# A table of distance biases: built on 8 or on 128 partitions, stored late or early

## The chip, the cores and the metric

The kernel runs on one core of a Trainium2 chip. The metric is the device time of one execution in microseconds (us), the median of several runs. A profile is one execution recorded by the hardware profiler; its span runs from the first to the last instruction of that execution. Engines are named as the profile names them: PE (TensorE matmuls), PEld (its weight loads), DVE (VectorE), ACT (ScalarE), POOL (GpSimd) and SP (SyncE, which issues nearly all DMAs; SPq in the rows is its queue).

## The reference, cut to what matters

Two transformer blocks run one after the other on 512 tokens of 1024 columns. The first has an attention branch with a distance bias:

```python
def first_block(x, ...):
    h = rms_norm(x, norm_gain)
    proj = h @ w_in                       # q, keys/values, gates, recurrent branch, merge gates
    y_a = nsa_mixer(q, k_cmp, v_cmp, k_slc, v_slc, k_win, v_win, br_gate, ..., rel_bias)
    y_b = rglru_mixer(...)
    return x + merge(y_a, y_b) @ w_out

def nsa_mixer(...):                       # 8 heads in 2 groups of 4, blocks of 128 queries
    # compressed, selected and window branch, each:
    s = einsum(q, k) + rel_bias[t5_bucket(dist)]      # dist = query position - key position
    p = masked_softmax(s, dist >= 0)                  # a key ahead of the query takes no part
    ...
```

`rel_bias` is a table of 32 buckets by 8 heads. A bias depends on the head and on the distance alone. The second block (a gated recurrence, differential attention and a mixture of 32 experts) reads `x` of the first.

## The kernel before, in words

Products are in float32, each as three products of operands split into a high part and a rest (`h`/`l`, 24 matmuls of 512 columns for a [128, 512] result). Weights come in tiles of 512 KB: `gr` (wa, wo), `gt` (wb), `ada_w` (the second block's modulation), `cw` (compression), later `wg` and `wd` of the experts; ACT or DVE make the high part (`gth`, `grh`) and DVE or POOL the rest (`gtl`, `grl`).

The instructions are first recorded in a plain order, by `block1`, `block2` and `moe`, and then issued in an order that a planner (`Plan.order`) sets: by a simple table of durations, each engine takes the first recorded instruction that is ready. So the place in the plain order is a priority, not a place in time. Every engine then runs its own list in order and stops at an instruction whose operand is not there. All instructions are issued by one line of `Plan.issue`, so every row of the profile says L409; rows are told apart by the names of tiles.

The plain order of the first block: `hT_first` (the hidden states and the q product), `qkv(0)` (q normalised and transposed), `compress_in`, `qkv(1)` (keys and values), `bias_tables`, `nsa_gates`, `compress`, and then four rounds r = 0 to 3 of `silu2`, `bias(r)` and `nsa(r)`, two heads each; after these the recurrent branch.

`bias_tables` (line 830) makes, for each head, a row of 640 negated biases over all distances: a matmul of `rb` (32 buckets by 8 heads) with `oh` (a one-hot table of bucket by distance), in two pieces, and on DVE the negated sum with `far` (1e30 where the key lies ahead). The row stands on 8 partitions (`tab`, a tile of the size class t4). One DMA from these writes it to DRAM (`Rd`, [8, 128, 640]) 128 times per head, a copy for each query of a block. `bias(r)` reads it back with rows of 639 elements apart, so that each query's copy is shifted by one: `B`, [128 queries, 512 keys], one DMA for each of the 8 heads. From `B` DVE makes `cbias` (the bias of the compressed keys) and adds `B` to the scores of both other branches (`P<-b,B`).

A DMA of SP waits until the DMA that was issued eight before it has landed. A tile of a size class waits for the last use of the tile that had its buffer.

Of the kernel before, what the change touches and what calls it, by code (L numbers as in the profile page):

```python
# [47 lines left out]
class View:  # L48
    """A part of a planned tile: a stand-in access pattern, and the steps to it from the whole tile."""
# [45 lines left out]
    def box(self):  # L95
        """partitions, range of elements and, where the tile has rows, range in a row."""
# [31 lines left out]
class Offset:  # L128
    """Row offsets of an indirect DMA."""
# [49 lines left out]
class Plan:  # L179
    """Records the instructions of a program in a plain order, then issues them in an order in which every  # L180
    engine, by a simple model of its speed, always takes the first recorded instruction that is ready.  A tile
    is taken ahead of the plain order only where its tag has a buffer to spare up to its place in it."""
# [24 lines left out]
    @contextmanager  # L207
    def together(self):
        """the instructions of the body, all on one engine, stay in one piece."""
        self.grouped = []  # L210
        yield
        g, self.grouped = self.grouped, None
        self.record([(g[0][0][0][0], [x[0][0][1:5] for x in g], None, None, None, sum(x[0][0][5] for x in g), None, False)],
                    [v for x in g for v in x[1]], [v for x in g for v in x[2]])

    def record(self, alts, writes, reads, load=False):
# [9 lines left out]
        for v in reads:  # L226
# [5 lines left out]
            if v.t.space == "psum":  # L232
                # engines take turns at a bank
                deps.update(k for _, k in v.t.reads if len(alts) + len(k.alts) > 2 or k.alts[0][0] != alts[0][0])
# [230 lines left out]
def shares(eng, meth, outs, ins):  # L465
    """whether an instruction holds the ports of the SBUF that DVE and Pool share: Pool's that read it, DVE's with
    two inputs from it, and those that use both of its ports for one."""
# [8 lines left out]
def price(self, eng, meth, args, kw):  # L476
    """Nanoseconds that an instruction holds its engine, roughly."""
# [30 lines left out]
class Net:  # L508
# [16 lines left out]
    SIZES = {"t4": 38, "a2": 15, "p2": 9, "vm": 4, "sq128": 3, "c1k": 4}  # L525

    def start(self):
        """a plan for the instructions that follow; tiles kept by the one before stay where they are."""
# [48 lines left out]
    def pair4(self, name):  # L577
        """four [128, 512] operands of split products."""
# [9 lines left out]
    def slab(self, src, name="w", scale=None):  # L588
        """[128, 1024] of weights: high part and rest; scale: factors of 512 columns."""
# [13 lines left out]
    def mm3(self, ps, pairs, byk=False):  # L603
        """ps = sum over (lhs hi, lhs lo, rhs hi, rhs lo)."""
# [11 lines left out]
    def rsqrt(self, v, n, scale, out=None):  # L616
        """v -> (v * scale + EPS) ** -0.5 on [p, n], in a new small tile or in out."""
# [25 lines left out]
    def constants(self):  # L643
# [11 lines left out]
        # the table of functions, ahead of the data  # L655
# [12 lines left out]
    def load_rows(self, src, name):  # L668
        """the four chunks of rows."""
# [5 lines left out]
    def norm_rows(self, x):  # L675
        """x * rstd, token major."""
# [8 lines left out]
    def new_hT(self, src=None):  # L685
        """hidden states, transposed and split; src: 32 more columns, multiplied on the way."""
# [7 lines left out]
    def hT_first(self):  # L694
        """the hidden states of the first block, without 1 / rms: those factors (r1 per token, R as a row on all
        partitions) go to what is computed from them."""
# [52 lines left out]
    def scaled(self, out, ps):  # L749
        """out = ps / rms in the first block, ps in the second."""  # L750
# [36 lines left out]
    def narrow(self):  # L787
        """the 32 more columns, token major: psum [128, (chunk, 32)]."""
# [8 lines left out]
    def gemm_t(self, src, name="gt"):  # L797
        """columns on partitions: psum [128 cols, 512 tokens]."""
# [7 lines left out]
    def group(self, src, name="gr", scale=None):  # L806
        """split operands of 512 columns; src [4, 128, 1024] (pairs of k tiles)."""
# [6 lines left out]
    def gemm_part(self, ps, grp, c, lhs_hi, lhs_lo, ks):  # L814
        """adds the products of k tiles ks to ps."""
# [6 lines left out]
    def gemm_r(self, grp, c, lhs_hi, lhs_lo, byk=False):  # L822
        """tokens on partitions: psum [128 tokens of chunk c, 512 cols]."""
# [6 lines left out]
    def bias_tables(self):  # L830
        nc, I = self.nc, self.I
        oh, R = self.t4("tab0")[:32, 0:640], self.t4("tab1")[:8, 0:640]
        nc.sync.dma_start(oh, I["oh"])
        rb = self.small([32, 8], "rb", bufs=1)
        nc.sync.dma_start(rb, I["rel_bias"])
        nc.sync.dma_start(R, I["far"].to_broadcast([8, 640]))
        for a, b in ((0, 512), (512, 640)):
            p = self.pst()
            nc.tensor.matmul(p[:8, :b - a], rb, oh[:, a:b], start=True, stop=True)
            nc.vector.scalar_tensor_tensor(R[:, a:b], p[:8, :b - a], -1.0, R[:, a:b], op0=OP.mult, op1=OP.add)  # L840
        # a row per query, so that rows of one less read as shifted
        Rd = self.tile("dram", [8, 128, 640], F32, "Rd")
        nc.sync.dma_start(Rd, R.unsqueeze(1).to_broadcast([8, 128, 640]))
# [6 lines left out]
    def bias(self, r):  # L850
        """negated bias of the two heads of r, [query of a block, key], and that of the compressed keys."""
# [16 lines left out]
    def qkv(self, grp, acc=None, W=None):  # L868
        """q (grp 0) or the keys and values (grp 1): normalised, transposed; values token major."""
# [121 lines left out]
    def silu2(self, ps, name):  # L991
        """2 * silu of a psum tile."""
# [8 lines left out]
    def split_into(self, hi, lo, src, scale):  # L1001
        """hi + lo = src * scale."""
# [4 lines left out]
    def cmp_attention(self, r):  # L1007
        """weights over the compressed keys, times the gate, transposed: [(chunk % 2, g, key), (chunk // 2, query)]."""
# [73 lines left out]
    def lru_setup(self):  # L1082
# [7 lines left out]
        # softplus(-lambda)  # L1090
# [48 lines left out]
    def conv(self, up, wname, bname, i, nt):  # L1139
        """causal depthwise convolution along the tokens of a [128, 512] tile."""  # L1140
# [9 lines left out]
    def log1p(self, out, y, z, q):  # L1150
        """out = log1p(y) for y in [0, 1]; z, q scratch."""
# [10 lines left out]
    def gate_tile(self, wg, i):  # L1162
        """tanh(x / 2) of one tile of merge gates."""
# [8 lines left out]
    def merge(self, wg, g0, wp, a_hi, a_lo, b_hi, b_lo):  # L1172
        """sigmoid gates over two projections, split for the output product."""
# [25 lines left out]
    def block1(self):  # L1199
        nc, I = self.nc, self.I  # L1200
        self.qT, self.kT, self.V, self.mg = [], [], [], {}
        self.qkv(0, self.hT_first())
        self.compress_in()
        self.qkv(1, W=self.group(I["wa1"][1]))
        self.bias_tables()
# [35 lines left out]
    def modulation(self):  # L1241
        """One step per row tile of w_ada; the sections are shift1, scale1, gate1, shift2, scale2, gate2."""
        nc, I = self.nc, self.I
        for s in (1, 0, 2, 4, 3, 5):
# [11 lines left out]
            # sums over the partitions: four groups of 32 equal rows, 256 columns each  # L1256
# [29 lines left out]
    def conv_silu2(self, idx, i):  # L1286
        """2 * silu(conv(.)) of column tile idx."""
# [10 lines left out]
    def prefix(self, p, tri, ones, v, n):  # L1298
        """sums over the tokens up to each one; v [128, (chunk, n)]."""
# [6 lines left out]
    def mgates(self):  # L1306
        """per token and head: a = i - F, exp(-(F + M)); and the rows of M."""
# [83 lines left out]
    def rope_tables(self):  # L1391
        """cos and sin of position * inv_freq, [128, 4 chunks, 8]."""
# [33 lines left out]
    def qk_diff(self, grp, wname, scale, name):  # L1426
        """rms-normalised, rotated, transposed; one [128 = 2 maps x 64, 512] tile per head."""
# [36 lines left out]
    def diff(self, qT, kT, vd, after):  # L1464
        nc = self.nc
        # lam
# [125 lines left out]
    def route_setup(self):  # L1592
        """router weights with the modulation in them, and what the shift adds to the logits."""
# [27 lines left out]
        # per token: its number, weights over the experts  # L1621
# [16 lines left out]
    def route_chunk(self, c, h, x):  # L1638
        """half of the columns of x2 of a chunk: transposed for the router; with the second half, its logits."""
# [29 lines left out]
    def rest_chunk(self, c):  # L1669
        """what the high part leaves of the normalised rows."""  # L1670
# [10 lines left out]
    def route(self, lo, hi):  # L1681
        """group, two experts of it and their weights, per token of some chunks; places in the order of the tokens."""
# [8 lines left out]
        # first place of the largest group logit  # L1691
# [232 lines left out]
def layout(a):  # L1924
# [63 lines left out]
    for m in range(512):  # L1988
        oh[_bucket(dist)[m], m] = 1.0
# [18 lines left out]
```

## Time and profile before

| | us |
|---|---|
| runs (3) | 1157.68, 1158.07, 1160.14; median 1158.07 |
| span of the profiled execution | 1157.3 |
| PE busy in it | 1080.1 (93%) |
| DVE / ACT / POOL busy | 653.8 / 405.3 / 189.7 |
| DMA, mean over the span | 188 GB/s |

The profile gives the span as that execution's own time. It lies 0.8 us under the median of the runs, and what an execution has around its span is not shown apart. PE's busy time includes matmuls that wait in its pipeline, so 93% is not 93% of PE's peak. The section on rows below names what is read from the trace.

### The profile page before, as it was taken

The numbers are of one execution on the slowest core, as the hardware profiler recorded it, in microseconds if no ns is written. First come the engines' busy times: TensorE is split into PE (matmuls) and PEld (weight loads), VectorE is DVE, ScalarE is ACT, GpSimd is POOL, SyncE is SP. The second block draws the span as 40 slices with busy tenths as digits, with TensorE's granted clock in tenths as the row PEclk, the third lists the DMA queues.
The fourth block names the chain that finished last, engine by engine and source line by source line (L and its number), as shares of the span: only waits on it lengthen the run. The fifth ranks groups of instructions, "written<-read, shape, count | busy, mean of one in ns | idle before, by whom it ended". The sixth has DMA issues, their size and how long they took to land.

```text
span 1157.3 us, 15019 instructions
## 1 busy us (share of the span) xinstructions
PE 1080.1 (93%) x5414; PEld 757.7 (65%) x5414; DVE 653.8 (56%) x1459; ACT 405.3 (35%) x824; POOL 189.7 (16%) x180
## 2 busy tenths in 40 slices
PE   7994299999999999999999999999999999999995
PEld 6773167777788777777677887788787444444431
DVE  4841288989656474776978786544717322333221
ACT  6320166756222243634663342222325111111120
POOL 2300033200111122420130201100204101111011
PEclk9996599999999999999999999999999999999998
DMA  9635810113443471815044322545966999999981
GB/s 346 227 88 87 247 46 20 37 56 95 131 143 119 163 255 53 296 37 220 10 158 157 129 86 73 178 131 156 354 264 219 349 387 363 371 385 367 389 292 26
DMA packets 74506, 217.22 MB, mean 188 GB/s; under 512 B 10820, under 2 KB 12428, under 8 KB 74424
## 3 DMA queue, kind: packets, MB, share of 16 engines
q1 hardware_dynamic: 72120, 211.98, 52.5%
q0 software_dynamic: 2304, 4.20, 2.1%
q8 instruction: 45, 0.74, 0.3%
q14 instruction: 37, 0.30, 0.1%
HBM read 204.56 MB, written 15.22 MB: 190 GB/s over the span
## 4 chain that ended last, share of the span: by engine, by line
PE 60%; DMA 14%; issue 11%; DVE 9%; SPq 2%; ACT 2%; another core or an unknown queue 1%; POOL 0%; POOLq 0%; DVEq 0%; ACTq 0%
PE b L409 59%; DMA out_rows<-Y,si 11%; SPq L409 2%; PE H L409 1%; DVE P L409 1%; DVE dP L409 1%; DMA gr<-in_wo 1%; DMA gr<-in_wa 1%; DMA B<-Rd 1%; DVE ada_acc L409 1%; ACT grh L409 1%; DVE grl L409 1%; DVE dq L409 0%; DVE uc L409 0%
## 5 line engine op out<-in xcount | busy, mean ns | idle before, releaser
L409 PE MATMUL b<-hTh,gth 128*128 128x512 f32 x464 | 124.5, 404 | 0.0
L409 PE MATMUL b<-hTh,gtl 128*128 128x512 f32 x464 | 121.1, 399 | 0.0
L409 PE MATMUL b<-hTl,gth 128*128 128x512 f32 x464 | 119.3, 395 | 0.0
L409 PE MATMUL H<-wg,XT 128*64 128x512 f32 x512 | 114.8, 596 | 0.0
L409 PEld LDWEIGHTS b<-hTh,gth 128*128 128x128 f32 x464 | 86.8, 190 | 22.2 <-issue 3.5
L409 PEld LDWEIGHTS b<-hTh,gtl 128*128 128x128 f32 x464 | 87.0, 189 | 20.5 <-issue 1.6
L409 PEld LDWEIGHTS b<-hTl,gth 128*128 128x128 f32 x464 | 86.4, 188 | 19.4 <-issue 0.9
L409 POOL TENSOR_TENSOR gtl<-gt,gth 128x1024 fp32r<-128x1024 f32 x23 | 56.4, 2455 | 247.0 <-ACT gth L409 222.4
L409 PEld LDWEIGHTS H<-wg,XT 128*64 128x64 f32 x512 | 35.0, 137 | 68.5 <-issue 59.5
L409 DVE SCALAR_TENSOR_TENSOR ada_acc<-ada_w,cols,ada_acc 128x1024 f32<-128x1024 f32 x42 | 60.3, 1435 | 7.5 <-DMA ada_w<-in_w_ada 7.5
L409 POOL DMA_INDIRECT out_rows<-Y,si x16 | 25.0, 1563 | 236.0 <-DVE Y L409 203.0
L409 PE MATMUL b<-grh,hTh 128*128 128x512 f32 x192 | 57.1, 410 | 6.0 <-ACT grh L409 6.0
L409 PE MATMUL b<-kT,qT 64*128 64x128 f32 (+3 forms) x128 | 26.4, 515 | 36.0 <-DVE nst L409 35.9
L409 PE MATMUL b<-wd,aT 128*64 128x512 f32 x256 | 58.4, 598 | 1.5 <-ACT aT L409 1.5
L409 ACT ACTIVATE gth<-gt 128x1024 fp32r<-128x1024 f32 x54 | 56.4, 1049 | 6.7 <-DMA gt<-in_wb 6.6
L409 DVE SCALAR_TENSOR_TENSOR act<-act,H 128x256 f32<-128x256 f32 x32 | 13.4, 420 | 79.6 <-ACT act L409 79.1
L409 PE MATMUL b<-grl,hTh 128*128 128x512 f32 x192 | 57.0, 405 | 0.0
L409 POOL TENSOR_TENSOR grl<-gr,grh 128x1024 fp32r<-128x1024 f32 x15 | 39.4, 2635 | 100.0 <-ACT grh L409 87.6
L409 ACT ACTIVATE P<-P,nst 128x128 f32<-128x128 f32 (+3 forms) x64 | 35.3, 553 | 57.2 <-DVE nst L409 57.0
L409 PE MATMUL b<-grh,hTl 128*128 128x512 f32 x192 | 55.3, 400 | 0.0
L409 DVE SCALAR_TENSOR_TENSOR Y<-b,wt,gate 128x512 f32<-128x512 f32 x32 | 24.0, 750 | 49.8 <-PE b L409 49.4
L409 DVE TENSOR_TENSOR gtl<-gt,gth 128x1024 fp32r<-128x1024 f32 x35 | 42.6, 1222 | 14.8 <-ACT gth L409 13.1
(380 smaller groups left out, 1973.6 us busy)
## 6 DMA issues: line engine op xcount, KB each, us to landing
wg<-in_wgu SPq DMA_DIRECT2D x128, 512.0 KB
wd<-in_wd SPq DMA_DIRECT2D x128, 256.0 KB
gt<-in_wb SPq DMA_DIRECT2D x58, 512.0 KB
ada_w<-in_w_ada SPq DMA_DIRECT2D x48, 512.0 KB
gr<-in_wa SPq DMA_DIRECT2D x23, 512.0 KB
wp<-in_wp SPq DMA_DIRECT2D x16, 512.0 KB
gr<-in_wo SPq DMA_DIRECT2D x16, 512.0 KB
cw<-in_cmp_w SPq DMA_DIRECT2D x8, 512.0 KB
```

What stands on the lines that cost most here:

```text
L409: i = getattr(getattr(self.nc, eng), meth)(*[val(a) for a in args], **{k: val(v) for k, v in kw.items()})
```

## The change

The table of biases is built on 128 partitions, 16 equal rows for each head. A DVE copy spreads `rb` to `rx` (32 buckets by 128 = 8 heads x 16), one matmul of `rx` with 512 columns of `oh` gives all 128 rows, DVE negates them into `tab`, and POOL fills the other 128 columns of `tab` with 1e30, in place of a second matmul and the `far` table. The store then goes out from 128 partitions, eight copies from each. `Rd` and its readers are unchanged. `bias_tables` is recorded right after `hT_first`, ahead of `qkv(0)`. The rest of the diff takes out comments and docstrings, which emit nothing.

```diff
     def bias_tables(self):
         nc, I = self.nc, self.I
-        oh, R = self.t4("tab0")[:32, 0:640], self.t4("tab1")[:8, 0:640]
-        nc.sync.dma_start(oh, I["oh"])
+        oh, R = self.t4("tab0")[:32, 0:512], self.t4("tab1")[:, 0:640]
         rb = self.small([32, 8], "rb", bufs=1)
         nc.sync.dma_start(rb, I["rel_bias"])
-        nc.sync.dma_start(R, I["far"].to_broadcast([8, 640]))
-        for a, b in ((0, 512), (512, 640)):
-            p = self.pst()
-            nc.tensor.matmul(p[:8, :b - a], rb, oh[:, a:b], start=True, stop=True)
-            nc.vector.scalar_tensor_tensor(R[:, a:b], p[:8, :b - a], -1.0, R[:, a:b], op0=OP.mult, op1=OP.add)
-        # a row per query, so that rows of one less read as shifted
+        nc.sync.dma_start(oh, I["oh"])
+
+        rx = self.sq128("rx")[:32, :]
+        nc.vector.tensor_copy(rx.rearrange("p (h i) -> p h i", i=16), rb.unsqueeze(2).to_broadcast([32, 8, 16]))
+        p = self.pst()
+        nc.tensor.matmul(p, rx, oh, start=True, stop=True)
+        nc.gpsimd.memset(R[:, 512:640], BIG)
+        nc.vector.tensor_scalar(R[:, 0:512], p, -1.0, None, op0=OP.mult)
+
         Rd = self.tile("dram", [8, 128, 640], F32, "Rd")
-        nc.sync.dma_start(Rd, R.unsqueeze(1).to_broadcast([8, 128, 640]))
+        nc.sync.dma_start(Rd.rearrange("h (i r) m -> (h i) r m", r=8), R.unsqueeze(1).to_broadcast([128, 8, 640]))
         self.Rd = Rd
...
     def block1(self):
...
-        self.qkv(0, self.hT_first())
+        acc = self.hT_first()
+        self.bias_tables()
+        self.qkv(0, acc)
         self.compress_in()
         self.qkv(1, W=self.group(I["wa1"][1]))
-        self.bias_tables()
```

In the host layout `oh` shrinks to 512 columns and `far` goes. Since the planner orders anew, other instructions move too, on every engine, up to the recurrent branch; from there on the lists are the same.

On SP the store stood behind the weights of the attention rounds, with the first `B` eight issues later and `vbd` (values of the compressed keys) behind it. Before:

```order
L409 DMA gt<-in_wb 128x1024
L409 DMA Rd<-tab_276 1024x1x640
L409 DMA gt<-in_wb 128x1024
L409 DMA ada_w<-in_w_ada 128x1024
L409 DMA gt<-in_wb 128x1024 x2
L409 DMA ada_w<-in_w_ada 128x1024
L409 DMA gt<-in_wb 128x1024 x2
L409 DMA B_766<-Rd 128x512
L409 DMA B_779<-Rd 128x512
L409 DMA vbd<-vbd 64x128
```

Now it stands among the compression's weights, ahead of the copies of `kcT`, and four `B` stand ahead of the first weights of the rounds:

```order
L409 DMA wd<-in_wd 128x512
L409 DMA Rd<-tab_78 1024x1x640
L409 DMA cw_406<-in_cmp_w 128x1024
L409 DMA kcS<-kcT 64x512 x2
L409 DMA cw_440<-in_cmp_w 128x1024
L409 DMA cw_469<-in_cmp_w 128x1024
L409 DMA kcS<-kcT 64x512 x2
L409 DMA B_518<-Rd 128x512
L409 DMA B_533<-Rd 128x512
L409 DMA B_559<-Rd 128x512
L409 DMA B_575<-Rd 128x512
L409 DMA b_627<-in_cmp_b 64x256 x2
```

So the store moved ahead of three `cw`, four `gt` and one `ada_w`, and of the four copies `kcS`; the reads of `Rd` moved ahead of all weights of the rounds, and `vbd` (not in the rows) moved behind seventeen of these, `gt` and `ada_w`.

On DVE the first reader of `B` stood behind all of the compression and the first gate (`gn`). Before:

```order
L409 COPY kcT<-b 128x64
L409 TENSOR_TENSOR sx<-b,R 128x512
L409 SCALAR_TENSOR_TENSOR gn_829<-gn_829,sx 128x512
L409 TENSOR_SCALAR cbias<-B_766 128x7
L409 TENSOR_SCALAR cbias<-B_766 128x15
```

Now it stands ahead of the last sums of squares (`ssq_qk`) of the keys and of the first rests of `gt`:

```order
L409 TENSOR_REDUCE ssq_qk<-sqk 128x4
L409 TENSOR_TENSOR blk_162<-kcT,cols 64x8x31
L409 TENSOR_SCALAR cbias<-B_518 128x7
L409 TENSOR_SCALAR cbias<-B_518 128x15
L409 TENSOR_SCALAR cbias<-B_518 128x23
L409 TENSOR_SCALAR cbias<-B_518 128x31
L409 TENSOR_SCALAR cbias<-B_533 128x7
L409 TENSOR_SCALAR cbias<-B_533 128x15
L409 TENSOR_SCALAR cbias<-B_533 128x23
L409 TENSOR_SCALAR cbias<-B_533 128x31
L409 TENSOR_REDUCE ssq_qk<-sqk 128x4
L409 TENSOR_TENSOR gtl<-gt,gth 128x1024 x2
```

So a late `B` would now hold up DVE before the keys are normalised, where before it held up DVE behind them.

## Rows read from the trace of the kernel before

**Rows 1.** The page: busy time of PE, and its chain by line.

```profile
PE 1080.1 (93%) x5414; PEld 757.7 (65%) x5414; DVE 653.8 (56%) x1459; ACT 405.3 (35%) x824; POOL 189.7 (16%) x180
...
PE b L409 59%; DMA out_rows<-Y,si 11%; SPq L409 2%; PE H L409 1%; DVE P L409 1%; DVE dP L409 1%; DMA gr<-in_wo 1%; DMA gr<-in_wa 1%; DMA B<-Rd 1%; DVE ada_acc L409 1%; ACT grh L409 1%; DVE grl L409 1%; DVE dq L409 0%; DVE uc L409 0%
```

**Rows 2.** Waits from 0 to 300 us: total us, times, longest us.

```profile
DVE cbias L409 <- DMA B<-Rd: 44.1, 1, 44.1
...
PE b L409 <- DVE nst L409: 35.9, 1, 35.9
```

**Rows 3.** Chain of work, 90 to 140 us: start us, us, what.

```profile
89.88 11.31 PE b L409 x45
...
126.84 9.53 DMA B<-Rd
...
136.40 0.43 DVE cbias L409 x4
```

**Rows 4.** SP's timeline, 0 to 140 us: start us, us, DMA issued, times.

```profile
55.27 1.10 SPq L409 DMA_DIRECT2D gt<-in_wb  x1
72.90 0.82 SPq L409 DMA_DIRECT2D Rd<-tab  x1
73.82 5.40 SPq L409 DMA_DIRECT2D gt<-in_wb  x1
79.31 18.16 SPq L409 DMA_DIRECT2D ada_w<-in_w_ada  x1
...
126.84 1.58 SPq L409 DMA_DIRECT2D B<-Rd  x2
```

**Rows 5.** Stretches: length, busy us (instructions) by engine, clock, DMA share, GB/s.

```profile
core 0: us, PE busy (x) PEld busy (x) DVE busy (x) ACT busy (x) POOL busy (x), PEclk, DMA share, GB/s
101.20:137.10 35.90, 0.02 (x1) 0.02 (x1) 0.70 (x7) 0.04 (x1) 0.00 (x0) 0.53 0.69 159
90.00:97.00 7.00, 7.00 (x28) 5.41 (x28) 1.38 (x2) 0.63 (x1) 0.00 (x0) 0.52 0.46 50
137.10:144.90 7.80, 7.80 (x28) 5.12 (x29) 6.12 (x38) 5.26 (x21) 2.68 (x7) 0.52 1.01 392
20.00:40.00 20.00, 20.00 (x96) 15.64 (x95) 9.80 (x11) 12.98 (x20) 11.27 (x7) 1.00 0.83 314
```

**Rows 6.** Instructions of tile `tab`: duration ns min/median/max, first and last start us, forms.

```profile
L409 PE MATMUL b<-tab,rb x4: 267/428/591, 70.6 to 71.6; 32*8 32x512 f32 x2, 32*8 32x128 f32 x2
L409 DVE SCALAR_TENSOR_TENSOR tab<-b,tab x2: 269/474/679, 71.7 to 72.6; 8x512 f32<-8x512 f32 x1, 8x128 f32<-8x128 f32 x1
```

**Rows 7.** Timelines of DVE, POOL, PE and ACT, 23 to 73 us, with idle time ahead.

```profile
25.14 1.23 DVE L409 TENSOR_TENSOR gtl<-gt,gth 128x1024 fp32r<-128x1024 f32 x1 [6.31 <-ACT gth L409]
...
34.27 0.68 DVE L409 COPY R<-b 128x512 f32<-128x512 f32 x1
...
37.34 1.21 DVE L409 TENSOR_TENSOR grl<-gr,grh 128x1024 fp32r<-128x1024 f32 x1
...
49.11 0.65 PE L409 MATMUL b<-ident,qtok 128*128 128x128 f32 x4 [1.40 <-DVE qtok L409]
...
66.24 2.01 ACT L409 ACTIVATE gth<-gt 128x1024 fp32r<-128x1024 f32 x2
...
72.28 0.40 DVE L409 TENSOR_REDUCE ssq_qk<-sqk 128x4 f32<-128x256 f32 x1
```

**Rows 8.** Stretches ahead of, in and behind the four rounds; columns as in rows 5.

```profile
60.00:73.00 13.00, 13.00 (x61) 9.82 (x61) 4.53 (x9) 5.01 (x11) 0.00 (x0) 1.00 0.14 57
...
88.00:90.00 2.00, 0.82 (x3) 0.43 (x3) 1.35 (x2) 0.00 (x0) 1.04 (x1) 0.99 0.47 51
137.10:157.80 20.70, 20.70 (x132) 13.87 (x132) 15.29 (x77) 14.16 (x47) 5.55 (x12) 0.82 0.55 206
157.80:218.00 60.20, 56.49 (x456) 40.16 (x452) 54.66 (x215) 40.67 (x114) 19.69 (x19) 1.00 0.04 10
880.00:1157.00 277.00, 259.16 (x1230) 117.64 (x1229) 91.29 (x220) 50.34 (x121) 32.08 (x26) 0.99 0.89 321
```

More of the change, by code (lines that the diff above doesn't have):

```diff
@@ L1984, in layout @@
     d["rows"] = np.concatenate([rows[k].reshape(-1) for k in ROWS])[None, :]
-    dist = 511 - np.arange(640)
-    oh = np.zeros((32, 640), np.float32)
-    for m in range(512):
-        oh[_bucket(dist)[m], m] = 1.0
+    oh = np.zeros((32, 512), np.float32)
+    oh[_bucket(511 - np.arange(512)), np.arange(512)] = 1.0
     d["oh"] = oh
-    d["far"] = np.where(dist < 0, np.float32(BIG), np.float32(0)).astype(np.float32)[None, :]
     return {k: np.ascontiguousarray(v) for k, v in d.items()}
```

## The prediction, made before the changed kernel ran

> **What bounds the kernel now.** The page shows PE busy for 93% of the span, and its chain is PE for more than half of its length, with B<-Rd, the read of the bias table, as an entry of its own [rows 1]. A kernel like this gets shorter only where PE stands still or runs slowly, so I looked at the waits next. In the first 300 us one wait stands out on two engines: DVE waits 44.1 us, once, for B<-Rd, and behind DVE PE waits 35.9 us, once [rows 2]. The chain says where: PE's work ends at 101.2 us, B lands at 136.4, and the first thing that DVE does then is cbias [rows 3]. SP's timeline says why. The store of the table (Rd<-tab) is issued at 72.9 us and the first read of it not before 126.8; the read needs the whole store landed, so the store takes about 126.8 - 73.7 = 53 us. The loads behind it crawl too (one issue takes 18.16 us) [rows 4]. From 90 to 97 us, with the store the main traffic, DMA moves 50 GB/s at a share of 0.46, about eight of sixteen engines; in two stretches of loads to 128 partitions it moves 314 and 392 GB/s [rows 5]. 2560 KB (2.62 MB) in 53 us is 49 GB/s, the same number. So the wait is the store's own slowness and its late issue. In the stretch from 101.2 to 137.1 no engine does anything worth naming [rows 5]: all of them are behind B.
>
> [...]
>
> **The change part by part.** The table itself. Before: two matmuls (their four entries, two of 512 and two of 128 columns, sit between 70.6 and 71.8, some 1.2 us of PE) and two DVE operations of 0.68 and 0.27 us [rows 6]. After: one matmul of 512 columns, by the same rows at most two entries of about 0.43, 0.86 us, so PE gains 0.3 us; one DVE negation of 128x512, priced by R<-b of the same form at 0.68 us [rows 7]; a DVE copy 32x128, between zero and that 0.68, and a POOL fill while POOL has nothing that others wait for. The DVE copy waits for rb, and behind it stands the first rest gtl, which waited 6.31 us for its own data anyway, until 25.14 [rows 7]. rb is queued ahead of that weight, so the copy is covered; if rb came later than that, each us would go straight to gtl. The two small loads rb and oh move ahead of two gt and four gr on SP: some 65 KB, 0.2 us of DMA at 314 GB/s, and less than before in all, since far is gone.
>
> The negation stands on DVE behind R<-b (34.27) [rows 7], and a grl of 1.21 us moves from POOL to DVE [rows 7], about 1.9 us more on DVE ahead of the normalised q. Against that four blk operations, which stand ahead of qtok now, move behind it, and with them the wait for kcS. PE waits 1.40 us at 49.11 for qtok [rows 7]. I take that wait as gone (-1.4); the bounds are 0.5 us of extra wait (1.9 less 1.4) and the whole 1.4 won.
>
> The store. It can be issued when the table is there, at about 36 us, and SP's loads ahead of it are done by about 37. Its duration is not in this trace; the bounds are the 53 us of now, at 49 GB/s, and 2.62 MB at 392 GB/s, 6.7 us. I take 8.3 us (314 GB/s, the rate of loads to 128 partitions at that time) [rows 5], since the new store spreads over 128 partitions as they do. Some 13 MB have been asked for ahead of it, at 314 GB/s 41 us, an estimate; so it lands near 50, and B for the first rounds, four reads of 256 KB behind it, by about 58. Who is behind it: the copies kcS and two cw, needed by operations that do not reach PE until 72.8; on SP, behind the four B, the biases of the compression and three gt, the first of which was needed at 66.24 by ACT [rows 7]. Loads end at 56 us today and SP is then idle to 72.9 [rows 4], so all of this has some 5 to 10 us of cover. If the store takes more than about 20 us, the cover is gone. cbias on DVE now stands ahead of ssq_qk and gtl, at about 60 us, and DVE has cover there: from 60 to 73 it is busy for 4.53 of 13 us [rows 8].
>
> The wait. With B there by 58, DVE can start the first round as soon as its scores are there, about 91 us. What is late next is PE itself. The two pieces of PE's work, 89.88 to 101.2 [rows 3] and the first round from 137.1 to 157.8 [rows 8], now stand together: the 35.9 us between them go. The second period at the lower clock goes too: 7.8 us at 0.52 would be 4.1 at full clock, 3.7 us less. The first one stays, since what comes ahead of it is unchanged.
>
> In that joined piece PE has fewer finished scores to work on. Its bounds: no wait at all, as in the round from 137.1 (PE busy 20.70 of 20.70), or waits as in the three later rounds, 60.2 - 56.49 = 3.7 us in three [rows 8]. I take 1 us. vbd stands behind 17 loads on SP now. Most of their buffers come free when the products of the keys end, where the bias matmuls start now, at 70.6 [rows 6]; vbd is wanted near 100, so I take zero.
>
> The sum: -35.9 - 3.7 - 1.4 - 0.3 + 1.0 = -40.3 us. The profiled execution would go from 1157.3 to 1117.0, and with the 0.8 us to the median, about **1118 us**. Everything behind is the same list, moved ahead: in the experts' stretch DMA is at a share of 0.89 [rows 8], but those loads wait for buffers, not for a time of day.
>
> [...]
>
> **The rivals.** *Only twice as fast*: each engine's pace is what limits the store (49 GB/s by eight engines, 6.1 each), so sixteen give 98 GB/s and 27 us. It lands near 66, B near 70. DVE stands at cbias until then; the gt behind B land near 74, their gtl ends near 78 instead of 70, and kT comes about 5 us later: 1123. For it: nothing shows that a partition and not an engine is slow. Against: the same engines carry 314 GB/s in loads.
>
> *As slow as before, only earlier* (the repeated rows, not the partitions, are slow): 53 us from 37 is 90, B at 93. DVE stands at cbias from 61 to 93; from ssq_qk (72.28) to the first round (about 90.5, from PE's 89.88) it has 18 us to go [rows 3, 7], so the first round starts near 113 instead of 137. But the 11 us of PE work from 90 to 101 are then still to do, and the weights behind B on SP come late (3 us more): 1157.3 - 24 + 11 + 3, near 1147.
>
> *The gain is swallowed later*: if the stretch of the experts, 277 us at 321 GB/s [rows 8], ran at a pace that started when it does now, nothing would be won: 1158. Against it: its loads wait for buffers that the earlier work frees.
>
> *Slower than before*: the lower clock holds through the rounds. It fell after two us with PE busy for 0.82 of them, and the new order puts few long matmuls between the softmax steps of the first round. In the four rounds PE is busy 77.2 us, of which 69.4 at full clock [rows 8]. Each us of these at half clock costs one us; from 41 us on (more than half of them) the change loses, and at the most it would be 1118 + 69 = 1187. Against it: the later rounds with their own waits hold 1.00 [rows 8].
>
> **How the numbers follow.** Forecast 0.80 (1107 to 1131), only twice as fast 0.09 (1123), as slow as before 0.03 (1147), swallowed 0.03 (1158), slower 0.04, rest 0.01. The range: at the low end, 9 us more if the first slow period (3.4), the wait from 88 to 90 (1.2) and the later rounds' waits (3.7) went too: 1109, less 2 for what the new order may save. At the high end, 1118 + 5 (second case) + 4 (waits in the joined piece) + 2 (wait for qtok, and its gain not had) + 2 for a read B of the second round that comes late behind its buffer: 1131. A measurement of this kernel can tell about 0.2% from no change (2.3 us). Faster: 0.80 + 0.09 + 0.03 + 0.01 = 0.93; same 0.03; slower 0.04.
>
> **What would show it.** Right: Rd<-tab issued near 37 us and the first B<-Rd within 15 us of it; no wait of DVE for B above 2 us; PE without a hole between 90 and 140; one period of lower clock in the first round, not two; a DMA share near 0.9 while the store runs. Wrong: a store that takes 25 us or more, with DVE idle ahead of cbias between 61 and 95; ssq_qk or kT later than 80 us; PE's clock at 0.5 in the later rounds; a gap in front of the experts that was not there.

## The result, and the profile after

The changed kernel takes 1127.1 us (median of 4 runs, 1123.0 to 1129.2) against 1159.1 us for the kernel before (1157.7 to 1161.5): a ratio of 0.971, 95% interval 0.969 to 0.973. The forecast was 1118, with a range from 1107 to 1131. So the sign and the range held, but of the 40.3 us of the sum 32.1 came in the profiled run (span 1157.3 before, 1125.2 after). Most of what follows is about the 8 us that are missing.

The profile page of the changed kernel answers [rows 1]: PE's share rises from 93% to 96%, and `B<-Rd` is no longer in the chain.

```profile
PE 1081.7 (96%) x5412; PEld 758.1 (67%) x5412; DVE 655.3 (58%) x1465; ACT 404.7 (36%) x827; POOL 182.7 (16%) x172
...
PE 65%; DMA 12%; issue 11%; DVE 8%; ACT 1%; POOL 1%; POOLq 0%; SPq 0%; ACTq 0%; DVEq 0%
```

SP's timeline (start us, us, what, times) answers [rows 4]. The store is issued at 35.6 us and the first read of its result at 48.9, so it takes at most 13 us in the thick of the weight loads.

```profile
35.57 0.64 SPq L409 DMA_DIRECT2D Rd<-tab  x1
...
48.92 2.07 SPq L409 DMA_DIRECT2D B<-Rd  x4
```

PE's waits from 0 to 300 us (total us, times, longest) answer [rows 2]. The 35.9 us are gone, and so is the wait for qtok of [rows 7]; what is left in the rounds is many small waits.

```profile
PE b L409 <- ACT grh L409: 6.2, 1, 6.2
PE b L409 <- DVE sc L409: 2.3, 2, 1.2
...
PE b L409 <- DVE PT L409: 1.6, 3, 0.6
PE b L409 <- POOL P L409: 1.2, 1, 1.2
```

The table by stretches (length, busy us of each engine with instructions, clock, DMA share, GB/s) answers [rows 5, 8]. DMA moves 327 GB/s while the store runs. The granted clock is at 0.50 once at the start of the first round, as forecast, and then again from 178 to 184 us, in the last round, where the kernel before had 1.00 throughout.

```profile
40.00:50.00 10.00, 10.00 (x53) 8.34 (x52) 8.59 (x21) 0.00 (x0) 0.00 (x0) 1.00 1.02 327
90.00:92.00 2.00, 2.00 (x12) 1.80 (x13) 1.09 (x3) 0.65 (x4) 0.31 (x1) 0.50 0.00 0
...
178.00:180.00 2.00, 1.61 (x7) 1.05 (x8) 1.95 (x5) 0.65 (x2) 1.43 (x1) 0.50 0.00 0
...
182.00:184.00 2.00, 2.00 (x9) 1.48 (x7) 1.40 (x4) 0.94 (x3) 0.01 (x1) 0.50 0.50 92
```

One more low stretch lies behind the rounds, at the products of the experts (length, PE busy, clock, DMA share, GB/s):

```profile
1096.00:1098.00 2.00, 2.00 (x8) 0.50 0.00 0
```

How far ahead of the kernel before is the new one at the same instruction? At the end of the first round (gn<-b,gn, 163.4 against 113.1) it is 50.3 us, at the last product of the recurrent branch (b<-uc,wbd, 283.4 against 248.2) 35.2, at the last xr (880.9 against 847.1) 33.8, at the last product of XT 32.8. The 50 are no gain: the kernel before ran 24 products of gn1 ahead of its hole [rows 3], and the new one still owes them there. At 248 us the debts are paid, so 5 of the missing 8 us are lost before that point and 3 behind it. Of these 3, 1.4 come ahead of the last xr; the other 1.7 are the low stretch near 1096 us: from the last xr to the end the changed kernel takes 278.1 us here, 275.9 when it was measured again (below), and the kernel before 276.4.

### The profile page after: what moved, and what is told of

The parts are those of the page before. It is cut to its first block, busy times and chain, and to the rows that moved or that the text cites. A ratio compares the mean times of both kernels' runs of the same rounds, so it can differ in the third digit from the quotient of the medians.

```text
span 1125.2 us, 15005 instructions
## 1 busy us (share of the span) xinstructions
PE 1081.7 (96%) x5412; PEld 758.1 (67%) x5412; DVE 655.3 (58%) x1465; ACT 404.7 (36%) x827; POOL 182.7 (16%) x172
## 4 chain that ended last, share of the span: by engine, by line
PE 65%; DMA 12%; issue 11%; DVE 8%; ACT 1%; POOL 1%; POOLq 0%; SPq 0%; ACTq 0%; DVEq 0%
PE b L409 64%; DMA out_rows<-Y,si 11%; PE H L409 1%; DVE P L409 1%; DVE dP L409 1%; DMA gr<-in_wo 1%; DVE ada_acc L409 1%; DVE uc L409 0%; PE np L409 0%; DVE lz L409 0%; ACT grh L409 0%; POOL rs_p L409 0%; DMA gr<-in_wa 0%; DMA wd<-in_wd 0%; DVE cst L409 0%
## 5 line engine op out<-in xcount | busy, mean ns | idle before, releaser
L409 DVE SCALAR_TENSOR_TENSOR ada_acc<-ada_w,cols,ada_acc 128x1024 f32<-128x1024 f32 x42 | 60.2, 1433 | 6.6 <-DMA ada_w<-in_w_ada 6.5
L409 POOL TENSOR_TENSOR grl<-gr,grh 128x1024 fp32r<-128x1024 f32 x14 | 35.4, 2536 | 100.5 <-ACT grh L409 88.4
L409 ACT ACTIVATE grh<-gr 128x1024 fp32r<-128x1024 f32 (+1 forms) x39 | 39.9, 1036 | 29.2 <-DMA gr<-in_wo 11.9
L409 DVE TENSOR_TENSOR gtl<-gt,gth 128x1024 fp32r<-128x1024 f32 x35 | 42.6, 1223 | 11.1 <-ACT gth L409 10.3
L409 DVE SCALAR_TENSOR_TENSOR mg<-mg,b 128x512 f32<-128x512 f32 x32 | 21.9, 686 | 43.4 <-PE b L409 43.4
```

The costliest lines, as they stand in the source:

```text
L409: i = getattr(getattr(self.nc, eng), meth)(*[val(a) for a in args], **{k: val(v) for k, v in kw.items()})
```

## Experiments

**Which half of the change does it: the shape of the store or its place?** Two kernels undo one half each. In the first the table is built and stored as in the changed kernel, but recorded at the old place:

```diff
         acc = self.hT_first()
-        self.bias_tables()
         self.qkv(0, acc)
         self.compress_in()
         self.qkv(1, W=self.group(I["wa1"][1]))
+        self.bias_tables()
```

> The table on 128 partitions and its store, but recorded at the old place, behind the products of the keys. Theory A, the shape of the store is the whole gain: issued at about 73 us as before, it lands 7 to 9 us later and B is there by about 87, ahead of the first round at 89 to 91: within 3 us of the changed kernel, 1123 to 1130. Theory B, the early place carries a part: the 1.4 us wait for qtok comes back, and the store and the reads of B collide with the loads of gt on the sync queue between 73 and 97 us, so that the first round starts 5 us late or more: 1131 to 1137.

The second has the old table on 8 partitions, moved to the new place by the opposite edit.

> The old table on 8 partitions and its slow store, but recorded ahead of the q/k/v projection. The store takes 53 us again and starts near 36 to 40, so it lands at 90 to 93 if nothing slows it; loads that stand behind it on the queues come late. Theory A, the second rival as the prediction worked it out: 1147, because 11 us of PE's work between 90 and 101 us are still to do. Theory B: these 11 us run while DVE waits for B and cost nothing, the hole of PE only shrinks from 35.9 to about 12 us: 1130 to 1138. Theory C: the store holds back the weights so much (it shares the engines with 13 MB of loads) that PE waits for weights from 40 us on and nothing is gained: over 1150.

Measured, together with the changed kernel once more:

> The changed kernel once more. Theory A, the stretch of low granted clock in the last round (177.8 to 185.5 us) belongs to the order of the instructions: it comes at the same instructions again, and the time is 1124 to 1129. Theory B, it comes by chance: it isn't there, the rounds are some 3.5 us shorter in this profile, and the times lie apart in two groups.

| table | recorded late | recorded early |
|---|---|---|
| 8 partitions | 1159.9 (the kernel before) | 1162.7, ratio 1.002 (1.001 to 1.004) |
| 128 partitions | 1118.3, ratio 0.964 (0.962 to 0.966) | 1126.0, ratio 0.970 (0.968 to 0.972) |

The shape is the whole gain, 42 us. The early place costs 8 us with the fast store and some 3 with the slow one. For the late store the mechanism of theory A holds, but its range (1123 to 1130) is missed on the fast side: at 1118.3 the kernel beats the changed one, which no theory had. Its store is issued at 72.0 us and the first B at 81.5, still ahead of the first round at 89.8.

```profile
72.00 0.62 SPq L409 DMA_DIRECT2D Rd<-tab  x1
...
81.50 2.84 SPq L409 DMA_DIRECT2D B<-Rd  x2
```

Early and slow wins nothing, and it is theory C, only that small copies and not weights come late. SP's issues behind the store crawl (two cw take 23.3 us), the first kcS is issued at 60.2 us instead of 41.3, DVE stands 42.6 us for it, and PE 26.1 us ahead of a product that reads blk (its row names no releaser, so that blk was what it lacked is read from the order). The rival that I had priced at 1147 left this out. SP's, DVE's and PE's timelines:

```profile
35.88 0.82 SPq L409 DMA_DIRECT2D Rd<-tab  x1
36.82 23.29 SPq L409 DMA_DIRECT2D cw<-in_cmp_w  x2
60.20 9.44 SPq L409 DMA_DIRECT2D kcS<-kcT  x2
```

```profile
94.28 0.56 DVE L409 TENSOR_TENSOR blk<-kcS,cols 64x248 f32<-64x248 f32 x1 [42.56 <-DMA kcS<-kcT]
```

```profile
97.48 1.08 PE L409 MATMUL H<-cw,blk 128*64 128x256 f32 x2 [26.13 <-issue]
```

In the profile of the repeated changed kernel (after_again) the stretch of low clock in the rounds is there again, but from 152 to 159 us, in the third round, and 178 to 182 is at 1.00. So neither theory fits as it was put: a stretch comes in both, but not in the same round. A stretch with little work of PE does not tell where: from 176 to 178 us PE is busy for 1.04 of 2 us in the first profile, and the clock is 0.50 behind it; from 178 to 180 it is busy for 0.87 of 2 in the second, and the clock stays at 1.00.

**Why is the new store fast?** A kernel of stores alone.

> Computes nothing of the block (a copy of x stands in for the output). It stores the same 2.62 MB table (1024 rows of 640) eight times, twice over, one store behind the landing of the one before, each time with other source partitions: 8 side by side (as in the kernel before), 8 that lie 4 apart, 8 that lie 16 apart, 16 side by side, 16 that lie 8 apart, 32, 64 and 128 side by side. Each source row is repeated so that the bytes are the same. The pace of the kernel before was 49 GB/s from 8 partitions, 6.1 GB/s for each. Theory A, each source partition has a pace of its own of 6.1 GB/s: 53, 53, 53, 27, 27, 13, about 8 and about 8 us, in this order. Theory B, the repeating of a row is slow: the time goes by the number of repeats alone, which gives the same numbers as A. [...]

SP's timeline, second pass. A start is also the landing of the store before it, so a duration is the distance to the next start, in the order of the text: 52.9, 14.4, 28.9, 27.3, 15.2, 14.4, 14.4 us. The last store, from 128 partitions, has none behind it in this pass; in the first pass it started at 179.28, so it took 8.4 us.

```profile
179.28 0.55 SPq L1912 DMA_DIRECT2D Rd<-R  x1
187.70 0.72 SPq L1912 DMA_DIRECT2D Rd<-R  x1
240.63 0.69 SPq L1912 DMA_DIRECT2D Rd<-R  x1
255.04 0.59 SPq L1912 DMA_DIRECT2D Rd<-R  x1
283.89 0.59 SPq L1912 DMA_DIRECT2D Rd<-R  x1
311.19 0.56 SPq L1912 DMA_DIRECT2D Rd<-R  x1
326.41 0.56 SPq L1912 DMA_DIRECT2D Rd<-R  x1
340.83 0.54 SPq L1912 DMA_DIRECT2D Rd<-R  x1
355.22 0.55 SPq L1912 DMA_DIRECT2D Rd<-R  x1
```

The steady stretches within them, clock, DMA share and GB/s behind the length: 8 side by side, 8 that lie 4 apart, 16 side by side, 128.

```profile
196.00:236.00 40.00, 1.00 0.47 51
244.00:252.00 8.00, 1.00 0.52 207
...
290.00:310.00 20.00, 1.00 0.94 102
...
356.00:362.00 6.00, 1.00 0.95 365
```

Eight partitions with the same 128 repeats take 52.9 us when they are neighbours and 14.4 when they lie 4 apart. That rules out A and B: here it is where the source rows lie that sets the time, not how many there are or how often each is read. And the two shares of 0.47 and 0.52 go with 51 and 207 GB/s, while 16 neighbours keep the engines busy (0.94) at 102: in these stores the busy share is no measure of bytes. How the place of the rows sets the pace was not shown; 8 rows that lie 16 apart take 28.9 us, twice as long as 8 that lie 4 apart.

**Where do the 8 us of the early place go?** First the order. In the changed kernel PE runs all scores of a round in one piece at its start and the rest of the products in one piece at its end. PE's timeline at the seam of the first two rounds: the piece of products, the piece of scores, and the wait behind it.

```profile
113.54 2.03 PE L409 MATMUL b<-hTh,gtl 128*128 128x512 f32 x8
115.41 1.00 PE L409 MATMUL b<-kcT,qT 128*128 128x64 f32 x8
116.34 3.91 PE L409 MATMUL b<-kT,qT 64*128 64x128 f32 x24
121.46 0.33 PE L409 MATMUL b<-ident,P 128*128 128x128 f32 x1 [1.22 <-POOL P L409]
```

With the late store the scores of the second round stand between products while the first round still runs (it ends at 124.7), and PE doesn't wait there:

```profile
116.29 0.71 PE L409 MATMUL b<-kT,qT 64*128 64x128 f32 x8
116.93 1.20 PE L409 MATMUL b<-hTl,gth 128*128 128x512 f32 x4
118.06 1.13 PE L409 MATMUL b<-kT,qT 64*128 64x256 f32 x8
119.13 1.66 PE L409 MATMUL b<-ident,P 128*128 128x128 f32 x12
```

Two kernels change the recorded order around the rounds and leave the early store alone. The first:

```diff
+        self.gn[0] = self.silu2(self.gemm_t(I["wb1"][2]), "gn0")
         for r in range(4):
-            self.gn[r] = self.silu2(self.gemm_t(I["wb1"][2 + r]), f"gn{r}")
+            if r < 3:
+                self.gn[r + 1] = ...
             self.bias(r)
             self.nsa(r)
```

> The changed kernel (early store from 128 partitions), but the product and gate gn of each head pair is recorded one round earlier, so that gn0 and gn1 stand ahead of the first round. In the kernel with the late store 24 products of gn1 ran at 94 to 101 us, ahead of most scores, and PE then waited 3.8 us in the rounds against 6.2 in the changed kernel. Theory A, the changed kernel loses by the order of its rounds (scores in one piece at a round's start, products in one piece at its end), and this order follows from the first round that can start at once: products recorded ahead break it up, waits of PE in the rounds fall to 4 us or less, 1119 to 1123. Theory B, the loss has another cause (buffers taken early by four reads of B, places of tiles): the order may change, the time stays at 1124 to 1129.

The second:

```diff
+        self.bias(0)
         for r in range(4):
+            now = self.B, self.cbias
             self.gn[r] = self.silu2(self.gemm_t(I["wb1"][2 + r]), f"gn{r}")
-            self.bias(r)
+            if r < 3:
+                self.bias(r + 1)
+            nxt = self.B, self.cbias
+            self.B, self.cbias = now
             self.nsa(r)
+            self.B, self.cbias = nxt
```

> The changed kernel, but B and cbias of a round are recorded one round ahead, so that the sync queue is not held by reads of B that wait for buffers (in the changed kernel it stood at two pairs of reads from 84.5 to 103.6 and from 106.0 to 130.7 us). Theory A, what the sync queue holds back (gt for the next products) costs the rounds: the pairs are issued earlier or block less, waits of PE in the rounds fall, 1119 to 1123. Theory B, the loads behind were not needed yet and only the order of PE counts: 1124 to 1129.

Measured: 1121.7 (ratio 0.966, 0.965 to 0.968) and 1121.4 (0.966, 0.964 to 0.967), both within theory A and some 4.5 us better than the changed kernel. The median of hTl,gth, which matters below, stays at 395 ns from 260 to 400 us in both. So the order of the rounds, with the clock that it was run at, carries about half of the 8 us. Which feature of it does is not settled: in the second kernel SP no longer stands at a pair of B reads (2.4 us, where the changed kernel had 19.1 and 24.8), and in the first the named waits of PE from 88 to 250 us add up to 9.4 us, more than the 7.9 of the changed kernel, against what theory A said. What fell in both is PE's busy time (1077.0 and 1078.9 against 1081.7), since neither profile has a stretch of low clock in its later rounds. That is not the order alone: the changed order was also profiled once without such a stretch (other_slots, below), with a span of 1122.3 us, against 1125.2 with it and 1120.0 and 1119.7 in these two. How much of the 4.5 us is order and how much the clock of the executions is open.

The other half lies mostly behind the rounds. From the last b<-uc,wbd to the last xr the changed kernel takes 598.9 us (599.4 when repeated) and the late store 594.4. Length, PE busy with instructions, clock, DMA share and GB/s, changed kernel first:

```profile
248.20:847.10 598.90, 590.50 (x2838) 1.00 0.45 155
```

```profile
244.80:839.20 594.40, 585.29 (x2833) 1.00 0.46 157
```

PE is busy 5.2 us less with the late store. Five products fewer are left to it there, some 1.2 us (eight take 2.03 us above); the other 4.0 are in the products themselves. The instructions of tile gth (duration ns min/median/max, first and last start), first of the kernel before, then from 260 to 400 us of the changed kernel and of the late store:

```profile
L409 PE MATMUL b<-hTl,gth x112: 387/389/398, 300.8 to 409.2; 128*128 128x512 f32 x112
```

```profile
L409 PE MATMUL b<-hTl,gth x112: 387/395/402, 265.9 to 375.4; 128*128 128x512 f32 x112
```

```profile
L409 PE MATMUL b<-hTl,gth x112: 388/389/398, 261.1 to 369.3; 128*128 128x512 f32 x112
```

I first tried to move the tiles by handing out the 38 buffers of 4 KB in the opposite order.

> The changed kernel with the same instructions in the same order on TensorE, but its 38 buffers of 4 KB handed out in the opposite order, so that the same tiles lie at other addresses. The 128x512 products of hTl and gth had a median of 395 ns in the changed kernel (both profiles) and 389 in the kernel with the late store, over 2300 products of this size a difference of 3 ns is 7 us. Theory A, the address of a tile sets this: the medians move (389 to 392 for some groups, or others get longer) and the time by 2 to 5 us either way. Theory B, the order or the traffic around sets it: medians and time stay, 1124 to 1129.

```diff
-            self.nc.tag(tag, space, [k for k in range(...) if k not in kept], self.make)
+            self.nc.tag(tag, space, [k for k in range(...) if k not in kept][::-1 if tag == "t4" else 1], self.make)
```

It took 1126.8 (0.972, 0.970 to 0.974), the medians at 395 as before. But a buffer gets its address when it is first used, whatever its number, and in the built program the same 46 of 72 large buffers have the same kind of address. So this run was a repetition of the changed kernel and tells nothing on addresses; it does tell, with the same order of instructions, that the rounds can run without a stretch of low clock (1.00 from 96 us to the tail).

The built programs show what differs. A small tile takes 32 bytes per partition, and a large buffer behind an odd number of them starts 32 bytes past a multiple of 64. The order of first use sets the addresses, and with the new order small tiles (rb among them, at 113,728, where the late store has it at 142,400) come elsewhere. The next kernels allocate these small tiles first and keep every instruction of PE in its place:

```diff
+        small = {}
+        for t in [t for x in self.out for t in x[1].births if t.space == "sbuf" and -(-t.row // 8) % 2]:
+            small.setdefault((t.tag, t.slot), t)
+        for t in small.values():
+            t.make()
+        # one pad of 32 bytes more, where their number is odd (left out in the third)
         for _, nd, (e, eng, meth, args, kw, dur, _, _) in self.out:
```

> The changed kernel with every instruction in the same order on TensorE, but the buffers of 1 KB and more per partition start at multiples of 64 bytes. In the built program of the changed kernel 46 of 72 such buffers start at 32 past a multiple of 64 (the table's small tile rb of 32 bytes is allocated ahead of them now), in the kernel before 23 and in the kernel with the late store 25. Theory A, this offset makes the 128x512 products longer: in the stretch from 260 to 400 us their medians are 395 ns in the changed kernel and 389 in the late one, and from the end of the rounds to xr (245 to 840 us) that was 4.5 us. Then the medians fall to 389 or less and the time to 1119 to 1123. Theory B, something else (instruction order, traffic) sets 395: medians and time stay, 1124 to 1129.

> The kernel with the late store and all but 3 of its 72 large buffers at multiples of 64 bytes, same order on TensorE. Theory A (the offset of the buffers sets the length of products): its 25 offset buffers cost it something too, 1 to 3 us: 1115 to 1118. Theory B: 1117 to 1121 as without it.

> The kernel with the late store and 69 of its 72 large buffers 32 bytes past a multiple of 64, same order on TensorE. Theory A: the products get longer in all stretches, medians of 395 and more, 5 to 10 us more than with the buffers at multiples of 64: 1121 to 1127. Theory B: 1117 to 1121.

| kernel | large buffers 32 past a multiple of 64 | us | without the edit | ratio (interval) |
|---|---|---|---|---|
| changed | 4 of 72 | 1121.1 | 46 of 72: 1127.1 | 0.967 (0.964 to 0.969) |
| late store | 3 of 72 | 1114.7 | 25 of 72: 1118.3 | 0.961 (0.959 to 0.963) |
| late store | 69 of 72 | 1113.5 | 25 of 72: 1118.3 | 0.959 (0.957 to 0.962) |

The medians from 260 to 400 us, changed kernel at multiples of 64 and late store 32 past them:

```profile
L416 PE MATMUL b<-hTl,gth x112: 389/389/404, 266.4 to 373.5; 128*128 128x512 f32 x112
```

```profile
L414 PE MATMUL b<-hTl,gth x112: 389/389/395, 261.1 to 368.3; 128*128 128x512 f32 x112
```

With the late store this group stood at 389 before the edit too; what it gained lies in others, here b<-grl,mh from 260 to 400 us, late store without the edit and then 32 past:

```profile
L409 PE MATMUL b<-grl,mh x32: 388/394/398, 381.6 to 398.6; 128*128 128x512 f32 x32
```

```profile
L414 PE MATMUL b<-grl,mh x32: 389/389/397, 380.7 to 397.5; 128*128 128x512 f32 x32
```

Addresses are the cause: same order, other places, 6.0 and 3.6 us. But theory A had the wrong one. With 69 of 72 buffers at an offset of 32 the late store is as good (1113.5 us) as with 69 at multiples of 64 (1114.7); with the mix of 25 and 47 it takes 1118.3. No kernel was built with the small tiles in front and the large buffers mixed, but the traces speak against the small tiles: with the addresses of the built program set beside each product, a 128x512 product is followed by the next after 227 ns (median) in all three aligned kernels, in the late store after 227 where its two operands have the same offset (2,143 products) and 234 where they differ (339), in the changed kernel after 231 (1,302) and 234 (1,201). The 231 shows that a product's own pair is not all of it; what else must differ was not tried. From the last b<-uc,wbd to the last xr the aligned changed kernel and the aligned late store take:

```profile
249.10:843.10 594.00, 584.30 (x2838) 1.00 0.45 157
```

```profile
244.90:834.80 589.90, 580.89 (x2833) 1.00 0.45 158
```

PE's busy time falls by 6.2 us in the one and 4.4 in the other, 2 to 3 ns for each of some 2,200 products of this size; in the first a low stretch of the clock (676 to 682 us) hides a part.

With the buffers aligned alike the late store is still 6.4 us ahead (1121.1 against 1114.7). That is the price of the early place in order and clock. By the medians the mix of addresses adds 6.0 - 3.6 = 2.4 us more than it costs the late kernel, by the profiles of the unaligned kernels the 4.0 above; each median is known to some 2 us, and the aligned changed kernel was profiled with three low stretches in its rounds, so this division is rough.

**Does the clock fall because PE stands still at a round's start?** The late store once more, with work repeated ahead of the waits of the third and fourth round:

```diff
-            for ... in (eng if isinstance(eng, list) else [(eng, meth, args, kw)]):
+            for ... in (eng if isinstance(eng, list) else [(eng, meth, args, kw)]) * again.get(id(nd), 1):
```

Here `again` is 2 for the last score product ahead of the transposes of sc, the second of these, and the transposes of P among the three instructions behind it. In the late store's profile the granted clock is 0.81 from 150 to 152 us and 0.50 from 152 to 158, by which some 3.4 us of work are lost (an estimate: 2 us x (0.19 + 3 x 0.50)), near the 3.6 that theory A takes.

> The kernel with the late store, and at the start of the third and fourth round TensorE repeats a score product and five or so transposes just ahead of its waits there (same inputs, same outputs, 3 us of work in all, of which about 2 lie in the waits). [...] Theory A, the clock falls because TensorE stood still there: no low stretch in the rounds, 3.6 us won less 1 of added work: 1114 to 1117. Theory B, it falls anyway: the low stretch stays and the time is 1119 to 1122.

> All that won so far together: the table on 128 partitions stored late, the repeated score products at the start of the third and fourth round, the large buffers at multiples of 64 bytes. If the gains add up (2.3 us for the repeats, 1 to 3 for the buffers): 1112 to 1115. If the repeats only won by chance (low granted clock comes and goes from execution to execution): 1115 to 1119.

They took 1116.0 (0.962, 0.961 to 0.964) and 1111.9 (0.959, 0.956 to 0.961): 2.3 and 2.9 us less than the same kernels without the repeats. The third round's start, first without the repeats (late_64) and then with them (late_fill), in columns length, PE busy, clock, DMA share and GB/s:

```profile
148.00:150.00 2.00, 0.63 (x4) 1.00 0.00 0
...
152.00:154.00 2.00, 1.63 (x8) 0.50 0.05 12
154.00:156.00 2.00, 2.00 (x8) 0.50 0.00 0
```

```profile
144.00:146.00 2.00, 1.24 (x9) 1.00 0.00 0
146.00:148.00 2.00, 1.67 (x11) 1.00 0.00 0
```

That is theory A's picture, and in both kernels with repeats no stretch of the rounds is low, where the three profiles of this order without them have one each at 150 to 158 us. I don't call it shown: PE still has gaps there (1.24 of 2 us at a clock of 1.00), and in the two kernels the low stretch at 90 to 97 us is gone as well, which lies ahead of the first repeated instruction. Each of the two profiles is also of the fastest run of its kernel, the gains of 2.3 and 2.9 us lie within overlapping intervals, and the mean granted clock of the runs is 0.991 to 0.994 with the repeats and 0.987 to 0.992 without. What decides whether it falls stays open. The last kernel, at 1111.9, is the fastest measured, some 48 us or 4% under the kernel before.

## Why the prediction was right, and where it missed

- **The store** (8.3 us, landing near 50, B by 58): right. It takes at most 13 us including the queue, 8.4 in the kernel of stores alone, and cbias starts at 62.1 without a wait. The reason that I gave, that 128 partitions spread as the loads do, fits: the store from them alone moves 365 GB/s. The second case, twice as fast, took the engines for the limit and fell: 8 neighbours reach 51 GB/s at a share of 0.47, and 8 that lie 4 apart reach 207 at 0.52, so the number of busy engines did not set the pace.
- **The hole of 35.9 us and the wait for qtok of 1.4**: both gone, as forecast.
- **The table's own matmul, -0.3**: nearly nothing. Its two entries take 1.12 us together (587 and 692 ns), not 0.86: the 0.43 was a median over entries of 512 and of 128 columns.
- **Waits in the joined rounds, +1.0**: too small. PE stands still for 6.6 us from 88 to 204.1, against 3.9 in the four rounds before (137.1 to 239), so 2.8 more. I had priced the first round only and taken the later ones as they were.
- **The second low period, -3.7**: the step that failed most, and with it the sign "one period of lower clock in the first round, not two". That the wait had brought it was my assumption, and no run shows it. It went from the first round, but in the profile another of the same length (some 3.4 us of work lost) came in a later round. Of the four profiles of this order one had none there, two had one, and one had three. The rival of low clock in the rounds was listed at 0.04 as a loss of the whole; it came as one stretch.
- **"Everything behind is the same list, moved ahead"**: the unpriced step. The instructions from the recurrent branch on are the same, but their tiles lie elsewhere: behind the rounds the median of hTl,gth rose from 389 to 395 ns, and PE is busy 1.3 us longer from the last b<-uc,wbd to the last xr (590.5 against 589.2), although the kernel before has a low stretch of the clock there (714 to 718 us).
- **The sum**: PE's idle time fell by 33.7 us (77.2 to 43.5) where the terms said 36.3, and its busy time rose by 1.6 (1080.1 to 1081.7) where they said 4.0 less. 2.6 and 5.6 are the 8.2 missing. The late store reaches what I had summed (idle 40.6, busy 1076.3, in all 40.4 less), though not term by term: its wait for qtok stays and a later low stretch comes there too.

The cover named for the store ("more than about 20 us, the cover is gone") is borne out by the slow early one, where PE stood for 26.1 us. That the range held the result is in part luck. Its high end adds a slower store, waits in the joined piece, a wait for qtok and a late read of B; of these only the second came, at 1.8 us more than the sum had, and the rest of the 8 us is clock and addresses, which the high end does not name. At the low end the three items listed add up to 8.3 us, not 9.

## To carry to other kernels

When a change alters a transfer and moves it too, price and try the two apart: here the shape of the store won 42 us and its earlier place lost 8 of them. In a kernel whose order and addresses follow from a plan, a small tile that moves can make many products behind it longer (395 ns against 389 for hTl,gth here), so compare the duration of the commonest instruction in both traces before looking for waits. For a store from a few rows, try partitions that lie apart: 8 of them took 14.4 us here at a distance of 4, 28.9 at 16 and 52.9 side by side.

## What was not expected of the hardware

The 128x512 product of hTl and gth takes 389 ns at the median where the large buffers start at one common offset, at multiples of 64 bytes or all 32 past them, and 395 in the changed kernel, where 46 of 72 have the one offset and 26 the other (389 in the late store, where 25 have the one and 47 the other); with one offset for nearly all buffers the kernels are 3.6 to 6.0 us faster. A store of 2.62 MB from 8 neighbouring partitions goes at 51 GB/s, and from 8 that lie 4 apart at 207. And the granted clock drops for 4 to 8 us in the rounds of the changed kernel at places that differ from one execution to the next of the same instructions, while the late store has its drop at 150 to 158 us in all three profiles of its order.
